# Where the split of the output weights begins, and which engine subtracts for the gating unit's first weights

## The chip, the cores and the metric

The kernel runs on one core of one Trainium2 chip. The metric is the device time of one execution in microseconds, lower being better. A core has a matrix engine (TensorE, PE in the profile; PEld is its weight load), a vector engine (VectorE, DVE), an engine for activations and copies (ScalarE, ACT), a programmable engine (GpSimd, POOL) and SyncE (SP), which here only issues transfers between the chip's memory and the on-chip buffers. Each engine takes its instructions in the order of its own queue and waits where an operand isn't there yet.

## What is computed

Two layers on 512 tokens of width 1024, all in float32. Each layer has a mixer and a dense feed-forward part, with RMS norms before and after each.

```python
def reference(x, norm_gains, ...):
    for i in range(DEPTH):                      # DEPTH = 2
        h = _rmsnorm(x, norm_gains[i, 0])
        h = _rwkv7_time_mix(h, ...) if i % 2 == 0 else _sgu_mixer(h, ...)
        x = x + _rmsnorm(h, norm_gains[i, 1])
        h = _rmsnorm(x, norm_gains[i, 2])
        h = _swiglu(h, ffn_w_gate[i], ffn_w_up[i], ffn_w_down[i])
        x = x + _rmsnorm(h, norm_gains[i, 3])
    return x

# time mixing: S_t = S_{t-1} diag(w_t) + (S_{t-1} a_t) b_t^T + v_t k_t^T ;  y_t = S_t r_t, 16 heads of 64
    ...
    return (y * g) @ w_o

# gating unit
    h = jax.nn.gelu(x @ w_in + b_in, approximate=False)
    u, v = jnp.split(h, 2, axis=-1)
    ...                                         # layer norm of v, s = masked block product of ws and v
    return (u * s) @ w_out
```

## The kernel before

**Precision.** A float32 product is made of three products of rounded halves: hi by hi, hi by lo, lo by hi (`mm3`, L206). Each weight tile therefore is loaded by SyncE into one of two `wraw` buffers (L188), cast to `whi` by ScalarE (L181) and its remainder `wlo = wraw - whi` subtracted by VectorE (L182, in `split`). With `pool=True` the cast is at L197 and GpSimd does the subtraction (L198). A `wraw` buffer is free again once its `wlo` is made.

**Stages.** The program runs through the time mixer (to about 460 us), the first FFN, the gating unit (from about 810 us, its first weights earlier), and the second FFN (from about 965 us).

**The time mixer** treats the 16 heads in four groups of four (b = 0 to 3). The recurrence is done in chunks of 64 tokens. For each group, `back(b)` inverts triangular 64 x 64 blocks, by 16 x 16 on VectorE (the loop that ends with the transposes Dn and Dt, L1054 and L1055) and then by two merges with small products on TensorE: Qp (L1071), Qs (L1074, VectorE), Np and Tp (L1080, L1083), copies to Dn2 and `bdT` (L1086, L1088), Q2p (L1094) with its copies Q2 (L1097, L1098), and T2p (L1103). The final merge is the pair of copies at L1107, by ScalarE for one head of a pair and by VectorE for the other. After it come four rounds of mp (L1112), the copy MVt (L1114, ScalarE), gh (L1119) and two sums on VectorE (L1121, L1122). The scan of group b (`scan(b)`) needs them: chunk by chunk, us (L1148), su (L1150 VectorE, L1153 ScalarE) and Yp (L1161). Its `su` tiles are four buffers in turn, each loaded by SyncE (L1133) as soon as the chunk four back is through.

**The output projection** (`out_proj`) multiplies the mixer's result `oT` by `w_o`, in units of 256 rows by 512 columns, 24 matmuls each, into four accumulators called `acc`. Its matmuls are available early, for the heads that are done, and fill gaps on TensorE during the last inverse and the last scan. The argument `after` holds traced instructions: every instruction that a unit issues on an engine is put behind those of them that are on that same engine.

**What sets the order.** The program is built with a scheduler that simulates the time line and from it chooses the order of each engine's queue. So an edge added at one place can move instructions anywhere behind it. The engines then follow the chosen order, whatever the real time.

**The gating unit** multiplies the normed rows by the second half of `w_in` first, in two halves of 512 columns with four weight units each. The normed rows `hT` come from the end of the first FFN: for each block of 128 tokens the sum of squares, then rm, rr, rt, ry on one column (L269 to L272, VectorE), the new x (L336), transposes on TensorE, and hT (L62 ScalarE, L64 VectorE).

**The second FFN** uses sums of weight blocks (wsum, L405) and of activations (tsum, split into `bc`) to save products. TensorE's accumulators there are called R, Q and Z.

Of the kernel before, what the change touches and what calls it, by code (L numbers as in the profile page):

```python
# [13 lines left out]
P = 128  # L14
T = 512
D = 1024
KT = D // P
# [115 lines left out]
class Trunk:  # L133
# [535 lines left out]
    def rwkv(self, x0):  # L669
        nc, i, tc = self.nc, self.i, self.tc  # L670
        v, a, g = nc.vector, nc.scalar, nc.gpsimd
        mm = nc.tensor.matmul
        with ExitStack() as ctx:
# [352 lines left out]
            def back(b, o):  # L1026
# [5 lines left out]
                bdT = inv[0]  # L1032
# [12 lines left out]
                for j in range(15):  # L1045
                    n = 15 - j
# [52 lines left out]
                T2p = self.bank("pt", "T2p")  # L1099
                for u in range(16):  # L1100
                    for hd in q2:
                        z = 64 * hd
                        mm(T2p[z:z + 32, u * 32:(u + 1) * 32], Q2[z + 32:z + 64, u, :], bdT[z + 32:z + 64, u, hd, 32:64],  # L1103
                           start=True, stop=True)
                for hd, cp in ((0, a.copy), (1, v.tensor_copy)):
                    z = 64 * hd
                    cp(bdT[z:z + 32, :, hd, 32:64], T2p[z:z + 32, :].rearrange("p (u t) -> p u t", t=32))  # L1107

                for hh, q in units:
                    mp, mt, mv, bx = self.bank("mp" if b else "pt", "mp"), MVt[hh, q], MV[hh, q], BX[hh, q]  # L1110
# [137 lines left out]
            xr, kr, ops, Y = None, {}, {}, {}  # L1248
            for n in PLAN:
                f, b = n[0], int(n[1])  # L1250
                if f == "P":
                    if xr is None:
                        xr = mixed_split(0, "ssssssss")
                    kr[b] = kr_proj(b)
                elif f == "E":
                    ops[b] = early(b, *kr[b])
                elif f == "X":
                    xs = mixed_split(2, XV)
                elif f == "V":
                    v_proj(xs, [b])  # L1260
                elif f == "F":
                    front(b, ops[b])
                elif f == "B":
                    back(b, ops[b])
                elif f == "S":
                    if b == 3:
                        GW.append(gate_weights(b))
                        OB.extend(bonus(b, ops[b]))
                    Y[b] = scan(b, ops[b], (lambda y: finish_half(b, ops[b], y, (0, 1))) if b == 3 else None)
                elif b == 3:  # L1270
                    finish_half(b, ops[b], Y[b], (2, 3))
                else:
                    finish(b, ops[b], Y[b])
# [15 lines left out]
            xts = [self.xp.tile([P, D], F32, name="x", tag="x", bufs=TT) for _ in range(TT)]  # L1289
            for t in range(TT):  # L1290
                nc.sync.dma_start(out=xts[t], in_=i["x"][0, t * P:(t + 1) * P, :])
            wo = i["rwkv_w_o"][0].rearrange("(u j p) n -> u p j n", p=P, j=2)
            norm = self.prenorm("g02")
            self.out_proj(acts, lambda u: wo[u], KT, i["norm_gains"][0, 1], xts, norm=norm, spare=e2, after=(ops[3]["turned"], ops[3]["copied"]))
            return xts, norm


    def sgu(self, xts, norm, nxt):
        nc, i = self.nc, self.i
        v, a, g = nc.vector, nc.scalar, nc.gpsimd  # L1300
        mm = nc.tensor.matmul
        w_in = i["sgu_w_in"][0]
# [16 lines left out]
        for half in range(2):  # L1319
            cols = slice(D + half * 512, D + half * 512 + 512)  # L1320
            hc = slice(half * 512, half * 512 + 512)
            acc = self.accs(1 - half)
            for u in range(4):
                hi, lo = self.weight(w_in.rearrange("(u j p) n -> u p j n", p=P, j=2)[u][:, :, cols], pool=half == 0)
                for j in range(2):
                    kt = 2 * u + j
                    for tt in range(TT):
                        tok = slice(tt * P, (tt + 1) * P)
                        self.mm3(acc[tt], (hT[kt][:, 0, tok], hT[kt][:, 1, tok]), (hi[:, j, :], lo[:, j, :]),
                                 kt == 0, kt == KT - 1)  # L1330
            for tt in range(TT):
                v.scalar_tensor_tensor(vt[tt][:, hc], acc[tt], norm.y[tt][:, 0:1], bv[:, hc], op0=ALU.mult, op1=ALU.add)
                s = self.sm.tile([P, 1], F32, name="vs", tag="vs", bufs=8)
                a.activation(vt[tt][:, hc], vt[tt][:, hc], AF.Gelu, accum_out=s)
                sums[half].append(s)
# [15 lines left out]
        for m in range(KT):  # L1351
            hi, lo = self.weight(w_in.rearrange("(kt p) n -> p kt n", p=P)[:, :, m * P:(m + 1) * P])
# [3 lines left out]
            u = uT[m // 2][:, m % 2, :]  # L1356
# [5 lines left out]
        acts = []  # L1362
        for m in range(8):
# [3 lines left out]
            t = self.sm.tile([P, T], F32, name="hn", tag="hn", bufs=2)  # L1367
# [6 lines left out]
        wo = i["sgu_w_out"][0].rearrange("(u j p) n -> u p j n", p=P, j=2)  # L1374
# [57 lines left out]
```

## Time and profile before

| what | us |
|---|---|
| median of 3 runs (lowest to highest) | 1325.09 (1322.51 to 1326.42) |
| the profiled execution's own time | 1323.67 |
| its span in the trace | 1322.0 |

The trace's mean granted TensorE clock is 0.979 of full speed. Times in what follows are counted from the start of the trace's span. In a row of the time line stand the start, the time, the engine, the line, the operation, output and inputs, and how many instructions the row joins; in brackets how long the engine had been idle ahead of it, and what it waited for.

### The profile page before, as it was taken

The page shows a single profiled execution, that of the slowest core. Times are in us where ns is not written, and L with a number is a line of the kernel's source. Part 1 is how long each engine was busy: PE and PEld are TensorE (multiplying, and loading weights), DVE is VectorE, ACT ScalarE, POOL GpSimd, SP SyncE. Part 2 cuts the span into 40 slices and gives each one's busy share as a digit, 9 for nine tenths or more (in the row PEclk, how much of TensorE's full clock was granted, in tenths as well). Part 3 has the DMA queues.
Part 4 walks back from the last instruction along what each step waited for, and adds up shares of the span by engine and source line. Part 5 has one row for each costly group of instructions (what it writes and reads, how often), then busy time and mean ns, then how long its engine had stood idle before and what let it go on. Part 6 is the DMA issues. An engine that isn't in the chain of part 4 may idle for free.

```text
span 1322.0 us, 24413 instructions
## 1 busy us (share of the span) xinstructions
PE 1260.2 (95%) x9644; PEld 1093.2 (83%) x9644; DVE 990.8 (75%) x1609; ACT 739.6 (56%) x1303; POOL 161.3 (12%) x304
## 2 busy tenths in 40 slices
PE   5999999989989899999999998999999999999998
PEld 3677798978867698999997877878888999998876
DVE  7975756477956687878779967476679877888985
ACT  7976884676543453445556546543454454556553
POOL 0000383566000002100000003020002000000000
PEclk9999999999889999999999999999989999999999
DMA  5137694322243225334353413343430433434322
GB/s 162 42 100 180 151 214 140 88 75 68 72 130 114 69 71 159 86 107 128 97 168 120 132 36 120 93 136 93 142 96 1 125 100 97 128 114 158 112 64 80
DMA packets 219379, 144.29 MB, mean 109 GB/s; under 512 B 67920, under 2 KB 193408, under 8 KB 219264
## 3 DMA queue, kind: packets, MB, share of 16 engines
q1 hardware_dynamic: 217968, 138.01, 36.3%
q0 software_dynamic: 1296, 4.72, 1.1%
q8 instruction: 76, 1.25, 0.4%
q14 instruction: 39, 0.32, 0.1%
HBM read 128.54 MB, written 14.16 MB: 108 GB/s over the span
## 4 chain that ended last, share of the span: by engine, by line
PE 65%; DVE 9%; ACT 2%; DMA 1%; issue 1%; SPq 0%; DVEq 0%; ACTq 0%
PE acc L206 25%; PE Q L206 10%; PE Z L206 7%; PE gu L206 7%; PE R L206 6%; PE u L206 3%; DVE wlo L182 1%; PE gh L1119 1%; DVE wsum L405 1%; PE lm L1004 1%; DVE x L336 1%; PE Yp L1161 1%; PE mp L1112 1%; DMA wraw<-in_rwkv_w_o_dram 1%; PE s L1366 1%
## 5 line engine op out<-in xcount | busy, mean ns | idle before, releaser
L182 DVE TENSOR_TENSOR wlo<-wraw,whi 128x1024 fp32r<-128x1024 f32 x79 | 98.7, 1249 | 72.2 <-ACT whi L181 71.8
L206 PE MATMUL Q<-bc,whi 128*128 128x256 f32 x816 | 147.3, 281 | 2.2 <-ACT hn L449 2.2
L206 PE MATMUL acc<-whi,ablk 128*128 128x512 f32 x448 | 141.6, 395 | 2.7 <-DVE acc L623 2.7
L181 ACT CAST whi<-wraw 128x1024 fp32r<-128x1024 f32 x79 | 82.8, 1049 | 103.2 <-PE acc L206 31.5
L206 PEld LDWEIGHTS Q<-bc,whi 128*128 128x128 f32 x816 | 125.6, 189 | 2.7 <-ACT hn L449 2.6
L181 ACT CAST whi<-wsum 128x1024 fp32r<-128x1024 f32 x68 | 71.0, 1051 | 87.6 <-DVE wsum L405 25.8
L206 PE MATMUL gu<-hT,whi 128*128 128x256 f32 (+1 forms) x448 | 112.8, 343 | 2.7 <-DVE hT L64 1.4
L206 PE MATMUL Q<-bc,wlo 128*128 128x256 f32 x408 | 114.5, 281 | 0.0
L206 PEld LDWEIGHTS acc<-whi,ablk 128*128 128x128 f32 x448 | 84.1, 188 | 23.3 <-ACT hn L621 1.8
L206 PE MATMUL Z<-bc,whi 128*128 128x256 f32 x544 | 99.8, 281 | 2.9 <-DVE bc L182 2.9
L206 PE MATMUL R<-bc,whi 128*128 128x256 f32 x544 | 98.7, 281 | 0.0
L182 DVE TENSOR_TENSOR wlo<-wsum,whi 128x1024 fp32r<-128x1024 f32 x68 | 82.2, 1220 | 19.1 <-ACT whi L181 18.1
L181 ACT CAST whi<-wq 128x1024 fp32r<-128x1024 f32 x51 | 53.5, 1050 | 76.0 <-PE gu L206 23.3
L206 PEld LDWEIGHTS gu<-hT,whi 128*128 128x128 f32 x448 | 79.5, 199 | 12.9 <-DVE hT L64 2.1
L206 PE MATMUL acc<-wlo,ablk 128*128 128x512 f32 x224 | 88.5, 395 | 1.4 <-DVE wlo L182 1.4
L206 PEld LDWEIGHTS Z<-bc,whi 128*128 128x128 f32 x544 | 84.0, 189 | 3.1 <-DVE bc L182 3.1
L206 PEld LDWEIGHTS R<-bc,whi 128*128 128x128 f32 x544 | 83.8, 188 | 0.3
L182 DVE TENSOR_TENSOR wlo<-wq,whi 128x1024 fp32r<-128x1024 f32 x51 | 63.6, 1251 | 26.9 <-ACT whi L181 26.8
L206 PE MATMUL proj<-xsp,whi 128*128 128x512 f32 x256 | 82.4, 401 | 1.3 <-ACT r L813 1.3
L206 PEld LDWEIGHTS Q<-bc,wlo 128*128 128x128 f32 x408 | 77.3, 189 | 0.0
L206 PE MATMUL R<-bc,wlo 128*128 128x256 f32 x272 | 76.6, 282 | 0.0
L206 PE MATMUL Z<-bc,wlo 128*128 128x256 f32 x272 | 76.3, 281 | 0.0
(379 smaller groups left out, 3219.3 us busy)
## 6 DMA issues: line engine op xcount, KB each, us to landing
wc<-in_ffn_w_down_dram SPq DMA_DIRECT2D x38, 512.0 KB, 3.8
wq<-in_ffn_w_gate_dram SPq DMA_DIRECT2D x68, 256.0 KB
wq<-in_ffn_w_up_dram SPq DMA_DIRECT2D x68, 256.0 KB, 4.5
wraw<-in_rwkv_w_rkv_dram SPq DMA_DIRECT2D x24, 512.0 KB, 5.2
wraw<-in_sgu_w_in_dram SPq DMA_DIRECT2D x16, 512.0 KB, 4.8
wraw<-in_ffn_w_gate_dram SPq DMA_DIRECT2D x10, 512.0 KB
wraw<-in_ffn_w_up_dram SPq DMA_DIRECT2D x10, 512.0 KB, 3.8
x<-in_x_dram SPq DMA_DIRECT2D x8, 512.0 KB, 3.3
```

The lines of the kernel that those rows point to most:

```text
L181: self.nc.scalar.copy(hi, src)
L182: self.nc.vector.tensor_tensor(lo, src, hi.bitcast(F32), op=ALU.subtract)
L206: self.nc.tensor.matmul(out, l, r, start=start, stop=stop, skip_group_check=resumed)
L336: v.scalar_tensor_tensor(xts[tt][:, c], f, y[:, 0:1], xts[tt][:, c], op0=ALU.mult, op1=ALU.add)
L405: v.tensor_tensor(s, x, y, op=ALU.add)
L1004: mm(lm[:, cc * P:(cc + 1) * P], st[:, cc].rearrange("p n t -> p (n t)"), mv[:, cc, :, hd, :], start=True, stop=True)
L1112: mm(mp[:, cc * P:(cc + 1) * P], bdT[:, q * NC + 4 * hh + cc].rearrange("p h t -> p (h t)"), mt[:, cc, :], start=True, stop=True)
L1119: mm(gh[:, cc * P:(cc + 1) * P], mt[rows, cc, :], bx[rows, 0:2, cc, :], start=True, stop=True)
L1161: mm(yp[yr, yc], MV[hh, q][:, cc, 1, hd, :], su[:, q, hd, :], start=True, stop=True)
L1366: mm(acc[:, tt * P:(tt + 1) * P], vt[tt][:, m * P:(m + 1) * P], wsT[:, m, :], start=True, stop=True)
```

## The change

Two edits. The final merge's copies at L1107 are remembered under `merged0` (ScalarE's) and `merged1` (VectorE's), and the mixer's output projection gets these two of the last group as `after`. So far it got the transpose Dt (L1055, VectorE, `turned`) and the last copy MVt at L1065 (ScalarE, `copied`), which both come before Qp. And in the gating unit the weights of the first half are no longer marked for GpSimd.

```diff
                 for hd, cp in ((0, a.copy), (1, v.tensor_copy)):
                     z = 64 * hd
-                    cp(bdT[z:z + 32, :, hd, 32:64], T2p[z:z + 32, :].rearrange("p (u t) -> p u t", t=32))
+                    o["merged" + str(hd)] = cp(bdT[z:z + 32, :, hd, 32:64], T2p[z:z + 32, :].rearrange("p (u t) -> p u t", t=32))
...
-            self.out_proj(acts, lambda u: wo[u], KT, i["norm_gains"][0, 1], xts, norm=norm, spare=e2, after=(ops[3]["turned"], ops[3]["copied"]))
+            self.out_proj(acts, lambda u: wo[u], KT, i["norm_gains"][0, 1], xts, norm=norm, spare=e2, after=(ops[3]["merged0"], ops[3]["merged1"]))
...
-                hi, lo = self.weight(w_in.rearrange("(u j p) n -> u p j n", p=P, j=2)[u][:, :, cols], pool=half == 0)
+                hi, lo = self.weight(w_in.rearrange("(u j p) n -> u p j n", p=P, j=2)[u][:, :, cols])
```

ScalarE's queue from the copy Dn2 of the last inverse to the casts behind its final merge; `whi` is the cast of an output weight, `Q_4547` is Q2, `su` and `Y` belong to the scan of group 2:

```order
 L1086 COPY Dn_4507<-Np 32x512 x2
-L1153 ACTIVATE su<-us,pc 64x64 x2
 L1088 COPY bdT<-Tp 32x16x32
 L1097 COPY Q_4547<-Q2p 32x512
-L181 CAST whi<-wraw 128x1024
 L1088 COPY bdT<-Tp 32x16x32
 L1153 ACTIVATE su<-us,pc 64x64 x2
-L181 CAST whi<-wraw 128x1024
+L1163 COPY Y<-Yp 128x256
+L1153 ACTIVATE su<-us,pc 64x64 x2
 L1107 COPY bdT<-T2p 32x16x32
+L181 CAST whi<-wraw 128x1024 x2
```

The two casts that stood ahead of the second bdT copy and of the merge copy now stand behind the latter. Two more casts that stood ahead of Qp's end have moved there as well, and the third and later ones stand between the MVt copies of the rounds.

SyncE's queue at the same place; `wraw` is the load of an output weight, `su` that of a scan tile (the last pair of group 2's and the first of group 3's), `g2r` a gate weight:

```order
 L1133 DMA su<-Vd 64x2x64 x2
-L188 DMA wraw<-in_rwkv_w_o_dram 128x2x512
-L1133 DMA su<-Vd 64x2x64 x2
 L1209 DMA g2r<-in_rwkv_g_dram 32x256 x3
-L188 DMA wraw<-in_rwkv_w_o_dram 128x2x512
-L1133 DMA su<-Vd 64x2x64 x2
-L188 DMA wraw<-in_rwkv_w_o_dram 128x2x512
-L1133 DMA su<-Vd 64x2x64 x2
+L1133 DMA su<-Vd 64x2x64 x8
+L188 DMA wraw<-in_rwkv_w_o_dram 128x2x512 x2
```

The loads of the third and the fourth output weight, which alternated with the su loads, now stand behind eight of these. The first two output weights are loaded long before in both versions.

VectorE's queue at the start of the gating unit, after the change, from the third token block's hn (`hn_9006`) to its row factor `ry_9013` and the first hT; `wlo_9260` and `wlo_9290` are two of the four remainders that GpSimd made before:

```order
L333 TENSOR_TENSOR hn_9006<-acc_8093,gain_8833 128x512
L269 TENSOR_SCALAR rm_9011<-ss_9007,rh_8858 128x1
L182 TENSOR_TENSOR wlo_9260<-wraw_9257,whi_9259 128x1024
L270 RECIPROCAL rr_9010<-rr_9010 128x1
L182 TENSOR_TENSOR wlo_9290<-wraw_9287,whi_9289 128x1024
L271 SCALAR_TENSOR_TENSOR rt_9012<-rr_9010,rm_9011 128x1
L333 TENSOR_TENSOR hn_9065<-acc_8094,gain_8833 128x512
L269 TENSOR_SCALAR rm_9070<-ss_9066,rh_8866 128x1
L270 RECIPROCAL rr_9069<-rr_9069 128x1
L272 SCALAR_TENSOR_TENSOR ry_9013<-rt_9012,rr_9010 128x1
L64 SCALAR_TENSOR_TENSOR hT_8972<-ptr_8980,vecT0_97,hT_8972 128x128
```

Before, rm, rr, rt and ry of this block followed each other, then came the two updates of x (L336) with that ry, and then the fourth block's hn, rm and rr and the first hT. Now two remainders stand among them and the two updates of x behind the first four hT. The third remainder stands some instructions ahead of this piece, the fourth behind the last ry.

VectorE's queue in the second FFN before the change, from one act product to the next; `bc_10956` is the remainder of a sum of activations, `wsum_11224` the sum of two weight blocks that are loaded there:

```order
L426 TENSOR_TENSOR act_10877<-sg_10944,R_10881 128x256
L405 TENSOR_TENSOR wsum_11224<-wq_11218,wq_11221 128x1024
L405 TENSOR_TENSOR wsum_11060<-wsum_11060,wq_10913 128x1024
L182 TENSOR_TENSOR bc_10956<-tsum_10953,bc_10955 128x1024
L405 TENSOR_TENSOR wsum_11287<-wq_10985,wq_11218 128x1024
```

And after it:

```order
L426 TENSOR_TENSOR act_10877<-sg_10944,R_10881 128x256
L405 TENSOR_TENSOR wsum_11060<-wsum_11060,wq_10913 128x1024
L182 TENSOR_TENSOR bc_10956<-tsum_10953,bc_10955 128x1024
L405 TENSOR_TENSOR wsum_11224<-wq_11218,wq_11221 128x1024
L405 TENSOR_TENSOR wsum_11287<-wq_10985,wq_11218 128x1024
```

`wsum_11224` has moved behind `bc_10956`. On TensorE the acc matmuls that lay between Qp and T2p, and between T2p and the first mp, have moved behind the first mp's start, all but one of them.

## The prediction, made before the changed kernel was timed

> **What bounds the kernel now.** I read the first part of the page, then windows of the stages, then the timeline engine by engine at each place the change touches. Last I read TensorE's waits.
>
> ```profile
> PE 1260.2 (95%) x9644; PEld 1093.2 (83%) x9644; DVE 990.8 (75%) x1609; ACT 739.6 (56%) x1303; POOL 161.3 (12%) x304
> 358.00:400.00 42.00, 35.77 (x673) 29.18 (x660) 23.13 (x46) 18.70 (x39) 1.11 (x3) 0.92 0.46 135
> 400.00:440.00 40.00, 39.43 (x249) 31.22 (x248) 21.59 (x47) 13.01 (x30) 0.00 (x0) 1.00 0.33 108
> ```
>
> TensorE is busy 95% of the span, so only its idle time and its stretches below full clock can be won. The windows (columns: length, then busy time of PE, PEld, DVE, ACT, POOL, then granted clock, DMA share, GB/s) show where that stands around the last inverse: 6.2 of 42 us idle at clock 0.92, then almost none. Whatever the stage gains by 400 us therefore lasts to 440. The change touches three such pockets: A, this inverse; B, the start of the gating unit; C, one place in the second FFN that only the scheduler moves.
>
> **A, the last inverse (355 to 420 us).** The inverse is a latency chain: Qp, Qs, Np and Tp, Q2p, T2p, the merge copies, then four rounds of mp, MVt, gh.
>
> ```profile
> 357.71 1.29 PE L1071 MATMUL Qp<-hn,LA 32*32 32x32 f32 x128
> 370.50 1.04 ACT L181 CAST whi<-wraw 128x1024 fp32r<-128x1024 f32 x1 [1.04 <-DMA wraw<-in_rwkv_w_o_dram]
> 371.56 0.58 ACT L1088 COPY bdT<-Tp 32x512 f32<-32x512 f32 x1
> 373.23 1.20 PE L1103 MATMUL T2p<-bdT,Q 32*32 32x32 f32 x64
> 376.83 1.04 ACT L181 CAST whi<-wraw 128x1024 fp32r<-128x1024 f32 x1 [4.15 <-DMA wraw<-in_rwkv_w_o_dram]
> 377.90 0.57 ACT L1107 COPY bdT<-T2p 32x512 f32<-32x512 f32 x1
> 382.86 1.16 PE L1112 MATMUL mp<-MVt,bdT 128*128 128x128 f32 x8
> 385.48 1.71 PE L1119 MATMUL gh<-BX,MVt 64*128 64x128 f32 x16 [0.85 <-ACT MVt L1114]
> 396.72 1.71 PE L1119 MATMUL gh<-BX,MVt 64*128 64x128 f32 x16
> ```
>
> Twice a cast of an output weight stands on ScalarE ahead of a copy of the inverse and waits for its load: 1.04 us before the bdT copy that T2p needs, 4.15 us before the merge copy. The change removes exactly this. Without the first cast (its 1.04 of wait and 1.04 of work) T2p comes about 2.1 us sooner, at 371.1. Without the second, ScalarE's merge copy (0.57) follows T2p's end (372.3) at once and ends at 372.9, where before it ended at 378.5. In the new order the first cast (1.04) and an acc matmul that needs it stand ahead of the first mp, so mp starts at about 374.0, where before it was 382.86: 8.9 us sooner.
>
> Not all of that is won. In the new order, no acc matmul runs between Qp and T2p any more; 33 of the 34 that run before the last gh now stand between the first mp and that gh, where none stood. Two of them at full clock and two at half clock:
>
> ```profile
> 398.94 0.63 PE L206 MATMUL acc<-whi,oT 128*128 128x512 f32 x2
> 399.41 0.39 PE L206 MATMUL acc<-wlo,oT 128*128 128x512 f32 x1
> 370.88 1.05 PE L206 MATMUL acc<-whi,oT 128*128 128x512 f32 x2
> 328.00:338.00 10.00, 10.00 (x131) 8.42 (x131) 9.63 (x25) 7.09 (x15) 3.90 (x8) 0.50 0.35 113
> 370.00:372.00 2.00, 2.00 (x5) 1.61 (x6) 1.13 (x3) 1.48 (x2) 0.41 (x2) 0.50 0.08 19
> 374.00:376.00 2.00, 2.00 (x46) 1.75 (x39) 0.00 (x0) 0.00 (x0) 0.00 (x0) 1.00 0.76 249
> ```
>
> At full clock two start 0.47 us apart (398.94 to 399.41), so 0.235 each; a pair takes 0.42 us more at half clock, 0.21 each. From the first mp to the end of the last gh before took 15.6 us (382.86 to 398.43), 0.85 of it the wait shown at gh, which an acc matmul now fills. After: 374.0 + 15.6 − 0.9 + 33 × 0.235 = 396.5, that is 1.9 us sooner, with 34 acc matmuls done where before had 24, so 10 × 0.235 = 2.3 less to do later. Gross gain 4.2 us.
>
> Two costs come off. **The clock**: with nothing but 32x32 and 64-wide matmuls from 359 to 372, I expect half clock to be granted when the acc matmuls begin. Before, the clock was at 0.50 from 370 to 372, though acc matmuls had begun, and full by 374; so I take 2.5 us at half, worth 1.2 us. By the rows this price has bounds of 0 and 5.0, the latter from the stretch 328 to 338 (the inverse before this one), where half clock lasted 10 us though TensorE is shown busy throughout. The Trainium skill, "TensorE: Matmul & The Clock Gate", section "What's actually happening", says the clock is halved after an idle window of about 3.4 us and full again after about 3.4 us of sustained activity; by it the price would be 1.7 us, so A 0.5 us smaller. The row 328 to 338 speaks against so short a recovery. **The third load**: SyncE takes its queue in order.
>
> ```profile
> 372.82 0.39 SPq L188 DMA_DIRECT2D wraw<-in_rwkv_w_o_dram  x1
> 383.00 2.87 SPq L1133 DMA_DIRECT2D su<-Vd  x4
> ```
>
> The load of the third output weight now stands behind eight su loads, and needs the wraw buffer that the first wlo frees. The last of those su loads waits for scan 2's chunk 6, which before let it go only at 383.00 and now stands on TensorE right behind T2p, at about 373. The first wlo ends at about 375.3, so the load issues then and lands 4.0 later (372.82 to 376.83), at 379.3. Its cast stands on ScalarE ahead of the second MVt and ends at 380.4; the mp that this MVt needs ends at about 381 (gh 2.6 us behind mp as before, 11 acc matmuls in place of the wait, then gh and mp). So nothing is lost by the rows, but the cover is thin, and I put 0.3 us. Behind these loads on SyncE stand su and hn loads which scan 3 needs only after 400, so they cost nothing unless the third load slips (third rival).
>
> A: −4.2 + 1.2 + 0.3 = **−2.7 us**; bounds −4.2 and +1.1 (clock price 5.0).
>
> **B, start of the gating unit (798 to 825 us).**
>
> ```profile
> L182 DVE TENSOR_TENSOR wlo<-wraw,whi 128x1024 fp32r<-128x1024 f32 x79 | 98.7, 1249 | 72.2 <-ACT whi L181 71.8
> 809.03 4.71 POOL L198 TENSOR_TENSOR wlo<-wraw,whi 128x1024 fp32r<-128x1024 f32 x2 [8.24 <-ACT whi L197]
> 818.08 2.37 POOL L198 TENSOR_TENSOR wlo<-wraw,whi 128x1024 fp32r<-128x1024 f32 x1 [1.40 <-ACT whi L197]
> 809.29 1.05 ACT L197 CAST whi<-wraw 128x1024 fp32r<-128x1024 f32 x1
> 807.19 0.16 DVE L272 SCALAR_TENSOR_TENSOR ry<-rt,rr 128x1 f32<-128x1 f32 x1
> 809.63 1.80 DVE L271 SCALAR_TENSOR_TENSOR rt<-rr,rm 128x1 f32<-128x1 f32 x1
> 811.47 2.29 DVE L272 SCALAR_TENSOR_TENSOR ry<-rt,rr 128x1 f32<-128x1 f32 x1
> 815.12 0.68 DVE L333 TENSOR_TENSOR hn<-acc,gain 128x512 f32<-128x512 f32 x1
> 815.91 1.11 DVE L64 SCALAR_TENSOR_TENSOR hT<-ptr,vecT,hT 128x128 fp32r<-128x128 f32 x4
> 818.10 2.37 DVE L272 SCALAR_TENSOR_TENSOR ry<-rt,rr 128x1 f32<-128x1 f32 x1
> 816.30 1.22 PE L206 MATMUL acc<-whi,hT 128*128 128x512 f32 x2 [3.44 <-DVE hT L64]
> 800.00:805.00 5.00, 5.00 (x24) 4.05 (x23) 1.40 (x5) 1.96 (x6) 0.79 (x1) 1.00 0.33 110
> 810.00:815.00 5.00, 2.86 (x21) 2.27 (x19) 4.93 (x4) 3.86 (x13) 3.74 (x2) 1.00 0.34 111
> 815.00:820.00 5.00, 3.70 (x10) 2.90 (x11) 5.00 (x14) 3.99 (x10) 2.50 (x2) 0.66 0.59 204
> ```
>
> Three VectorE instructions on one column, of 0.16 us at 807.19, last 1.80, 2.29 and 2.37, each while GpSimd runs one of the four subtracts and ending with it: about 6.0 us beyond that in which VectorE is held off, and it is the engine that TensorE waits for (3.44 us), at a clock of 0.66 afterwards. The change takes the subtracts off GpSimd and adds four of 1.25 to VectorE, 5.0 in all. One of these falls in 800 to 805, where VectorE is busy 1.40 of 5 us. Two stand between the third row block's L269 and L271, where the two long rows are gone; the last stands behind the last ry.
>
> Worked through in the new order from 809.5, just ahead of the first long row: two wlo are 2.5 (the second's cast ends at 810.34, in time); hn, rm and rr 0.8, as from 815.12 to 815.91; the other rr, rt and ry some 0.5. So the first hT starts at about 813.3 instead of 815.91. The two x updates (L336) that stood ahead of it now stand behind it. TensorE starts 2.6 us sooner, and with under 1 us idle instead of 3.44 the clock need not fall: (1 − 0.66) × 3.70 = 1.3 us more. Against that I put 0.4 us for x and the next hT coming tighter behind one wlo. B: −2.6 − 1.3 + 0.4 = **−3.5 us**; bounds −5.0 (nothing given back, the third long row worth a little more) and −1.0 (6.0 against 5.0, all serial).
>
> **C, second FFN (1028 to 1037 us).** Nothing in the diff speaks of it, but the order moves.
>
> ```profile
> 1029.58 0.41 DVE L426 TENSOR_TENSOR act<-sg,R 128x256 f32<-128x256 f32 x1
> 1032.62 1.23 DVE L405 TENSOR_TENSOR wsum<-wq 128x1024 f32<-128x1024 f32 x1 [2.62 <-DMA wq<-in_ffn_w_up_dram]
> 1033.76 1.22 DVE L405 TENSOR_TENSOR wsum<-wsum,wq 128x1024 f32<-128x1024 f32 x1
> 1034.90 1.22 DVE L182 TENSOR_TENSOR bc<-tsum,bc 128x1024 fp32r<-128x1024 f32 x1
> 1032.94 0.28 PE L206 MATMUL Q<-bc,wlo 128*128 128x256 f32 x1
> 1036.17 0.39 PE L206 MATMUL Z<-bc,whi 128*128 128x256 f32 x1 [2.95 <-DVE bc L182]
> ```
>
> The subtract for bc stands behind a sum that waits 2.62 us for a load; TensorE stands still 2.95 us for bc. In the new order the sum that waits stands behind bc. The second sum and bc then take 1029.95 to 1032.3, while TensorE's Q runs to 1033.2: the whole wait is covered. The sums behind are as early as before, and their casts and subtracts are due about 3 us sooner relative to TensorE, for which I give back 0.1. C: **−2.8 us**, bounds −2.95 and 0.
>
> **The sum.** −2.7 − 3.5 − 2.8 = −9.0 us. The profiled execution took 1323.67 us (span 1322.0), 1.4 below the median of 1325.09; on the median the same gain gives 1316.1, and I say **1316**. The other engines' orders are nearly the same elsewhere, so I put nothing there.
>
> **Rivals.**
> 1. **The clock eats A.** The acc matmuls that went are the only full-width ones between Qp and T2p. If half clock lasts 10 us, as at 328 to 338, A is +1.1 and the time 1325.1 + 1.1 − 3.5 − 2.8 = 1319.9. For: that row. Against: recovery by 374 before.
> 2. **VectorE stays the bound at B.** It is busy 4.93 and 5.00 of 5 us there, and 5.0 us are added against 6.0 removed. If all of it is serial, B is −1.0, and the time 1318.6. Against: one subtract falls into idle time and two x updates go behind hT.
> 3. **Slower: the third output weight comes late.** Its cast is ahead of the second MVt and its subtract ahead of the first gh sums, so each us of issue later than 376 moves three gh rounds by one, and a new standstill of TensorE costs up to 3.4 more (16 acc matmuls by 0.21) at half clock. With B and C as forecast, the gain is used up if the load issues at about 382 to 385, and it is slower by over 4 us from about 386 to 389. Before, the su loads now ahead of it went out at 383.00; 390 would give −9.0 + 14.0 + 3.4, or 1333. For: SyncE's queue is in order. Against: chunk 6 of scan 2 stands right behind T2p now, so it would have to be 10 us late by a wait that I don't see.
> 4. **The scheduler's gain at C is not there**, because the order follows simulated landings and another load binds next: C is 0, time 1318.9.
>
> **How the numbers follow.** Forecast 0.50, rivals 0.15, 0.12, 0.10 and 0.08, and 0.05 for two of the first, second and fourth together (about 1322). The range takes A, B and C to their good ends (−12.2, so 1313) with 3 us for the spread of runs (1322.5 to 1326.4), and at the other end everything short of the third rival: 1310 to 1325. About 0.3%, or 4 us, is what a measurement of this kernel can tell from no change. Faster by more than that: most of the forecast and of rivals 1, 2 and 4, 0.71; within it 0.18; slower 0.11.
>
> **What would show it.** A: in the timeline, no cast between Qp and the merge copies, the first mp at 374 rather than 383, the third wraw issue at 376, clock windows near 0.5 for 2 to 3 us from 372, the last gh near 396.5 with 34 acc matmuls done. B: L271 and L272 all near 0.2 us, TensorE's wait for the first hT under 1 us, clock 1.00. C: no wait of Z for bc at the place. It is wrong if TensorE waits between the first and second gh for a w_o load, if the clock stays at half past 380, or if the first Z wait comes back as a wait of another product within 10 us.

## The result and the profile after

The changed kernel took **1315.96 us** in the median of five runs (1312.98 to 1320.0), the kernel before 1325.44 (1322.51 to 1326.76). The ratio is 0.9933, 95% interval 0.9911 to 0.9956. The profiled execution took 1315.28 us with a span of 1313.6. So the forecast of 1316 was met, but in part by luck: of its three terms C was met, B came out better, and A, the inverse, brought little of what was forecast.

To see where the time went I cut each trace at the start of four rows: Qp of the last inverse, the first gu of the first FFN, the first wst of the gating unit, and its first s.

| stretch | before | after | difference | forecast |
|---|---|---|---|---|
| start to Qp | 357.71 | 356.53 | −1.2 | 0 |
| Qp to gu (place A) | 102.30 | 101.71 | −0.6 | −2.7 |
| gu to wst | 350.48 | 351.22 | +0.7 | 0 |
| wst to s (place B) | 99.94 | 95.39 | −4.5 | −3.5 |
| s to end (place C) | 411.57 | 408.75 | −2.8 | −2.8 |

**Place A.** First the timeline of the changed kernel, ScalarE's casts and copies and SyncE's load, then TensorE's rows:

```profile
371.89 0.57 ACT L1107 COPY bdT<-T2p 32x512 f32<-32x512 f32 x1 [0.95 <-PE T2p L1103]
372.49 1.99 ACT L181 CAST whi<-wraw 128x1024 fp32r<-128x1024 f32 x2
380.51 1.04 ACT L181 CAST whi<-wraw 128x1024 fp32r<-128x1024 f32 x1 [0.88 <-DMA wraw<-in_rwkv_w_o_dram]
383.33 0.59 ACT L1114 COPY MVt<-mp 128x512 f32<-128x512 f32 x1 [1.78 <-PE mp L1112]
361.36 13.27 SPq L1133 DMA_DIRECT2D su<-Vd  x8
374.82 1.53 SPq L188 DMA_DIRECT2D wraw<-in_rwkv_w_o_dram  x2
356.53 1.29 PE L1071 MATMUL Qp<-hn,LA 32*32 32x32 f32 x128
365.08 1.92 PE L1094 MATMUL Q2p<-Dn,LA 32*32 32x32 f32 x64 [0.18 <-ACT Dn L1086]
374.19 1.91 PE L1112 MATMUL mp<-MVt,bdT 128*128 128x128 f32 x8
397.27 1.71 PE L1119 MATMUL gh<-BX,MVt 64*128 64x128 f32 x16
```

No cast of an output weight stands ahead of the merge copy any more. From Qp to the first mp it is now 17.7 us, before 25.2. The third weight's load issued at 374.82, its cast waited for the landing, and the second MVt waited for its mp and not for that cast. Yet the last gh starts at 397.27, where it had been 396.72. The reason shows in the windows of the whole stretch and of pieces of it. The columns are the length, then busy time of PE, PEld, DVE, ACT and POOL, then granted clock, DMA share and GB/s. Before, Qp to gu, and two pieces of it:

```profile
357.71:460.01 102.30, 91.36 (x1002) 72.91 (x1000) 59.54 (x136) 43.05 (x100) 1.11 (x3) 0.95 0.35 108
368.00:372.00 4.00, 4.00 (x62) 3.46 (x57) 2.46 (x5) 2.54 (x4) 0.41 (x2) 0.61 0.40 137
380.00:384.00 4.00, 4.00 (x29) 2.97 (x28) 0.45 (x2) 0.78 (x4) 0.00 (x0) 0.68 0.38 131
```

After, the same stretch, and five pieces of it:

```profile
356.53:458.24 101.71, 92.93 (x1002) 75.47 (x1000) 59.96 (x136) 43.31 (x100) 1.10 (x3) 0.92 0.35 109
360.00:364.00 4.00, 2.91 (x180) 2.77 (x181) 1.53 (x4) 2.15 (x6) 0.00 (x0) 0.63 0.33 73
364.00:368.00 4.00, 3.34 (x90) 3.14 (x90) 1.65 (x3) 2.52 (x5) 0.00 (x0) 0.50 0.06 12
368.00:372.00 4.00, 4.00 (x89) 3.64 (x89) 0.98 (x2) 1.72 (x7) 0.41 (x2) 0.50 0.13 28
372.00:376.00 4.00, 3.75 (x27) 3.27 (x25) 3.33 (x4) 2.97 (x5) 0.00 (x0) 0.50 0.20 29
376.00:380.00 4.00, 4.00 (x17) 2.96 (x17) 0.35 (x1) 0.96 (x2) 0.00 (x0) 0.74 0.73 257
```

TensorE's idle time fell from 10.9 to 8.8 us (length less busy time), but the loss by the clock, busy time by one less the granted clock, rose from about 4.6 to 7.4 (7.8 with the clock unrounded). Half clock held from about 361 to 378, 17.1 us in one piece. Before, the clock had fallen too, but came back sooner: 3.4 us from 368.9, again 3.4 us from 379.1, and 3.4 us from 444.

**Place B.** The timeline of the changed kernel, VectorE and then TensorE, and two windows:

```profile
808.42 1.22 DVE L182 TENSOR_TENSOR wlo<-wraw,whi 128x1024 fp32r<-128x1024 f32 x1
809.63 1.21 DVE L182 TENSOR_TENSOR wlo<-wraw,whi 128x1024 fp32r<-128x1024 f32 x1
810.75 0.21 DVE L271 SCALAR_TENSOR_TENSOR rt<-rr,rm 128x1 f32<-128x1 f32 x1
811.67 0.14 DVE L272 SCALAR_TENSOR_TENSOR ry<-rt,rr 128x1 f32<-128x1 f32 x1
811.74 1.13 DVE L64 SCALAR_TENSOR_TENSOR hT<-ptr,vecT,hT 128x128 fp32r<-128x128 f32 x4
812.14 0.73 PE L206 MATMUL acc<-whi,hT 128*128 128x512 f32 x2 [0.30 <-DVE hT L64]
810.00:815.00 5.00, 4.70 (x29) 3.78 (x28) 5.00 (x16) 4.85 (x15) 0.54 (x1) 1.00 0.75 228
815.00:820.00 5.00, 5.00 (x25) 4.10 (x24) 4.76 (x18) 5.00 (x19) 0.00 (x0) 1.00 0.57 195
```

The long rows are gone, TensorE waits 0.30 us for the first hT instead of 3.44, and the clock stays at 1.00 where it was 0.66. VectorE is as full as before, now with work of its own.

**Place C.** VectorE's timeline in the second FFN, and TensorE's first Z that needs bc:

```profile
1024.78 1.22 DVE L405 TENSOR_TENSOR wsum<-wsum,wq 128x1024 f32<-128x1024 f32 x1
1025.92 1.22 DVE L182 TENSOR_TENSOR bc<-tsum,bc 128x1024 fp32r<-128x1024 f32 x1
1027.05 2.35 DVE L405 TENSOR_TENSOR wsum<-wq 128x1024 f32<-128x1024 f32 x2
1027.93 0.28 PE L206 MATMUL Z<-bc,whi 128*128 128x256 f32 x1
```

bc comes ahead of the sum that had waited, and Z runs without a wait in brackets.

### The profile page after: what moved, and what is told of

It reads as the page before. It is cut to its first block, busy times and chain, and to the rows that moved or that the text cites. A ratio compares the mean times of both kernels' runs of the same rounds, so it can differ in the third digit from the quotient of the medians.

```text
span 1313.6 us, 24404 instructions
## 1 busy us (share of the span) xinstructions
PE 1257.4 (96%) x9644; PEld 1091.1 (83%) x9644; DVE 988.1 (75%) x1613; ACT 739.4 (56%) x1303; POOL 151.6 (12%) x300
## 4 chain that ended last, share of the span: by engine, by line
PE 68%; DVE 7%; ACT 2%; issue 1%; DMA 1%; POOL 0%; DVEq 0%; ACTq 0%
PE acc L206 25%; PE Q L206 10%; PE gu L206 9%; PE R L206 7%; PE Z L206 7%; PE u L206 3%; DVE wlo L182 1%; PE gh L1119 1%; PE mp L1112 1%; PE Yp L1161 1%; PE lm L1004 1%; DVE wsum L405 1%; DVE x L336 1%; PE s L1366 1%; PE ptr L281 0%
## 5 line engine op out<-in xcount | busy, mean ns | idle before, releaser
L182 DVE TENSOR_TENSOR wlo<-wraw,whi 128x1024 fp32r<-128x1024 f32 x83 | 103.1, 1244 | 66.5 <-ACT whi L181 57.7
L181 ACT CAST whi<-wraw 128x1024 fp32r<-128x1024 f32 x83 | 86.9, 1050 | 101.5 <-PE acc L206 29.2
L206 PE MATMUL Z<-bc,whi 128*128 128x256 f32 x544 | 99.8, 281 | 0.0
L206 PEld LDWEIGHTS gu<-hT,whi 128*128 128x128 f32 x448 | 78.8, 197 | 13.7 <-ACT hT L62 2.4
```

Source lines behind the costliest of these rows:

```text
L181: self.nc.scalar.copy(hi, src)
L182: self.nc.vector.tensor_tensor(lo, src, hi.bitcast(F32), op=ALU.subtract)
L206: self.nc.tensor.matmul(out, l, r, start=start, stop=stop, skip_group_check=resumed)
```

## The experiments

**Each part alone, and more work for TensorE in the gap.** My theory from the two traces: part 1 wins time in the inverse and gives it back at half clock, since it takes away the only full-width products between Qp and T2p; B and C carry the result. The rival: part 1 is worth what the forecast said.

The first run has only part 1 (shown against the changed kernel):

```diff
-                hi, lo = self.weight(w_in.rearrange("(u j p) n -> u p j n", p=P, j=2)[u][:, :, cols])
+                hi, lo = self.weight(w_in.rearrange("(u j p) n -> u p j n", p=P, j=2)[u][:, :, cols], pool=half == 0)
```

> Only the output weights' split behind the merge copies; the gating unit as before (GpSimd subtracts for its first half). bc stands ahead of the waiting sum in the second FFN here too. Theory 1 (what part 1 wins in the chain it gives back at half clock): from Qp's start to the first gu of the first FFN 101.7 us as in the changed kernel (before 102.3), half clock for over 12 us within 358 to 380, GpSimd's long rows at the gating unit still there, the wait of Z for bc gone; time 3 to 4 us under before. Rival (part 1 is worth the 2.7 us of the forecast, the rest was luck): Qp to gu about 99.6, time 5.5 under before.

It took 1320.64 us (12 runs; before beside it 1326.80 in 17), ratio 0.9965 (0.9946 to 0.9985): 4.6 us under before by the ratio, give or take 2.6, and 6.2 by the medians. Qp to gu was 101.8 with 17.1 us at half clock, s to end 408.9. As C alone is 2.6 in this trace, some 2 us are left for A, with an interval that holds both 0 and the forecast. The stage and its clock speak for the theory, the time for neither.

The second has only part 2:

```diff
-            self.out_proj(acts, lambda u: wo[u], KT, i["norm_gains"][0, 1], xts, norm=norm, spare=e2, after=(ops[3]["merged0"], ops[3]["merged1"]))
+            self.out_proj(acts, lambda u: wo[u], KT, i["norm_gains"][0, 1], xts, norm=norm, spare=e2, after=(ops[3]["turned"], ops[3]["copied"]))
```

> Only the gating unit's subtracts on VectorE; the output weights' split as before. bc stands ahead of the waiting sum here too. Theory 1: Qp to gu 102.3 as before, first gu to the first s matmul of the gating unit 446.6 (before 450.4), from there to the end 408.8 (before 411.6); time 6.5 to 7.5 us under before, so hardly slower than the whole change. Rival (part 1 matters): 6.3 under before or less, and 2.7 us slower than the whole change run beside it.

The time was 1316.17 us (6 runs), the ratio 0.9924 (0.9898 to 0.9950), against 0.9924 (0.9898 to 0.9951) for the whole change on the same chip. That is some 10 us under before, where both theory and rival had said 7.5 at most. With B and C there, part 1 adds nothing that can be seen; but the six runs of each spread over 6 us, and by that spread I estimate that a gain of up to some 3 us could hide in it, so these times alone don't rule out the 2.7 of the forecast. Its profile held a surprise, though, in the windows of Qp to gu and of one piece:

```profile
355.32:463.45 108.13, 98.35 (x1002) 79.64 (x1000) 60.33 (x136) 43.16 (x100) 1.10 (x3) 0.87 0.33 102
384.00:396.00 12.00, 12.00 (x67) 10.76 (x65) 7.17 (x16) 2.85 (x6) 0.69 (x1) 0.50 0.40 133
```

In this execution the old order got half clock for 6.8 us from 365.1, as long as the two falls of before took together in the inverse, and then for 17.1 us more from 382.1, while TensorE was shown busy all through. The stretch took 108.1 instead of the expected 102.3. The same queue can end on either side, so a difference of single traces in this stage, A's −0.6 too, says little by itself. I take this as one source of the scatter of before, whose 17 runs beside these went from 1319.75 to 1331.31; that the other runs differ by this was not traced.

The third is the test of the clock by useful work. The first two weight units, loaded long before, keep the old points; the later ones go behind the merge copies (called two units early below):

```diff
-                for ins in after:
+                for ins in (after[0:2] if half == 0 and u < 2 else after[2:4] or after):
                     order.enter_context(self.tc.issue_after(ins.ins))
...
-after=(ops[3]["merged0"], ops[3]["merged1"])
+after=(ops[3]["turned"], ops[3]["copied"], ops[3]["merged0"], ops[3]["merged1"])
```

> The whole change, but the first two units of output weights, whose loads have landed long before, stay behind the old points (Dt, MVt) and only the later units go behind the merge copies. So full-width acc matmuls lie again between Qp and T2p and no cast that waits for a load stands ahead of a copy of the inverse. Theory 1 (it was the clock): half clock for under 6 us between Qp and the second gh, first mp within 17 us of Qp's start (17.7 in the changed kernel, 25.2 before), Qp to gu 99 or less, time 2 to 3 us under the whole change. Rival (the chain of the inverse was not the limit, scan 3 is): Qp to gu 101.5 to 102.5 whatever the clock, time as the whole change.

```profile
358.86:458.04 99.18, 89.90 (x1003) 72.53 (x1001) 59.75 (x136) 42.53 (x101) 1.10 (x3) 0.98 0.36 112
368.00:372.00 4.00, 3.30 (x100) 3.12 (x100) 2.18 (x4) 1.87 (x5) 0.09 (x1) 0.72 0.48 143
372.00:376.00 4.00, 4.00 (x82) 3.13 (x82) 0.45 (x2) 1.06 (x5) 0.32 (x2) 0.85 0.09 21
```

These windows are Qp to gu and the only two pieces below full clock: in sum 3.4 us at half (0.28 and 0.15 of 4 us, by two), where the change's trace had 17.1. TensorE's idle time is 9.3 us, no less than the change's 8.8; what has gone is most of the clock's loss, from 7.4 to 1.8. The time was 1311.54 us (1310.20 to 1312.29), ratio 0.9888 (0.9864 to 0.9911), and its slowest run is under the change's fastest (1313.27 beside it). That is 4.3 us under the change run beside it, more than the 2 to 3 expected. The first mp came 18.8 us after Qp, later than the 17 expected and than the change's 17.7, and the stage was shorter all the same. Not all of the 4.3 need lie in this stage: from gu to wst this trace is 3.0 us shorter than that of the change beside it, which has 6.8 us at half clock there and this one none.

The fourth was the change itself, on the same chip.

> The changed kernel itself, beside the others on the same chip, for the comparison and for the spread of its stages from run to run: 8 to 10 us under before, Qp to gu 101.2 to 102.2, half clock from about 361 to 378 again.

It took 1315.82 us (1313.27 to 1319.65), 10.1 us under before by the ratio. Qp to gu was 103.2, 1 us over what I expected; half clock came from 364.4 to 378.0, 13.7 us instead of 17. Qp started at 359.3 instead of 356.5: the traces of one kernel are up to 3 us apart before the inverse begins. One difference shows in all twelve traces of this case: the six in which Qp starts at 358.9 or later have a piece of half clock between 79 and 85 us (granted clock 0.72 there in this run), and the six in which it starts at 357.7 or earlier have none (1.00 in the change's first trace). Why the clock falls there in some executions is open.

**Work without use in the gap.** If it is the missing full-width work, products that nobody reads should keep the half clock short too. 28 were put where TensorE idles, once as products and once as transposes:

```diff
                 Qp = self.bank("pt", "Qp")
...
+                def filler(n):
+                    if b == 3:
+                        fill = self.ps.tile([P, 512], F32, name="fill", tag="b2", bufs=1)
+                        for k in range(n):
+                            mm(fill[:, 0:P], self.ident, self.ident, start=True, stop=True)
+
+                filler(8)
                 Qs = el("Qs", (P, 16, 32))
...
+                filler(10)
                 Q2p = self.bank("pt", "Q2p")
...
+                filler(10)
                 T2p = self.bank("pt", "T2p")
```

> The changed kernel with 28 products of the 128x128 identity by itself (float32, result never read) between Qp and T2p: 8 after Qp, 10 ahead of Q2p, 10 ahead of T2p, where TensorE is idle in the changed kernel. Nothing else is moved. Theory 1 (half clock comes of the missing full-width work): half clock for under 8 us within 356 to 384 (17 us in the changed kernel), Qp to first gu 100 or less though work is added, time 1 to 3 us under the whole change. Rival (half clock there depends on the small products themselves or on nothing here): half clock as long as in the changed kernel, Qp to gu 102 to 104, time 0 to 2 us over it.

Timeline and windows of it, first the three rows of filler (each product is two instructions):

```profile
360.59 2.05 PE L1077 MATMUL fill<-ident 128*128 128x128 f32 x16
368.13 3.60 PE L1077 MATMUL fill<-ident 128*128 128x128 f32 x20
373.20 2.50 PE L1077 MATMUL fill<-ident 128*128 128x128 f32 x20
359.37:463.39 104.02, 96.45 (x1059) 77.80 (x1057) 59.77 (x136) 42.91 (x100) 1.10 (x3) 0.98 0.34 106
```

The clock came out as expected (0.98 over the stretch, 3.4 us at half), the time did not: Qp to gu was 104.0, as the rival had it, and the kernel took 1317.96 us, ratio 0.9940 (0.9922 to 0.9959), no better than the change. The filler itself takes 8.2 us and lengthens the chain: Qp to mp is 20.1 us instead of 17.7. So full-width work in the gap keeps the half clock short, but here it paid only where it was work that had to be done anyway.

> The same 28 at the same places, but as transposes of the identity. In the kernel before, the stretch 328 to 338 was at half clock though TensorE ran 128x128 transposes through most of it. If transposes don't count as the full-width work that holds the clock: half clock for over 12 us and Qp to gu 102 to 104, while the products of the other run shorten it. If they count: as the products, within 0.5 us.

```profile
372.00:380.00 8.00, 8.00 (x134) 6.98 (x134) 1.67 (x3) 2.00 (x5) 0.33 (x2) 0.53 0.01 2
```

With transposes this 8 us window was nearly all at half clock, part of a piece of 10.2 us from 369.4, and the stretch had 0.94 on average, between the change's 0.92 and the products' 0.98. Qp to gu was 105.6, over both forecasts, in what was the slowest of the eight runs. But a transpose is one instruction and a product two, so there was also half as much work. Whether transposes count less as such stays open. The time was 1318.14 us (1311.92 to 1322.19), the ratio 0.9931 (0.9908 to 0.9955).

**GpSimd's hold.** Two of its four subtracts put back:

```diff
-[u][:, :, cols])
+[u][:, :, cols], pool=half == 0 and u in (1, 2))
```

> The changed kernel, but GpSimd again subtracts for the second and third unit of the gating unit's first half (L198 there twice instead of four times). If it is GpSimd's subtract that holds VectorE off: one or two of rt and ry (L271, L272) last over 1 us again, TensorE waits about 3 us for the first hT again, wst to s 98.5 to 100 (95.2 to 95.4 in the changed kernel, 99.9 before), time 3 to 4.5 us over the whole change. Rival (the order of the queue made the gain, not the hold): no long rows, wst to s 95 to 96.

```profile
807.46 4.72 POOL L198 TENSOR_TENSOR wlo<-wraw,whi 128x1024 fp32r<-128x1024 f32 x2 [47.70 <-ACT whi L197]
807.75 0.20 DVE L269 TENSOR_SCALAR rm<-ss,rh 128x1 f32<-128x1 f32 x1
807.87 0.15 DVE L270 RECIPROCAL rr<-rr 128x1 f32<-128x1 f32 x1
808.06 1.81 DVE L271 SCALAR_TENSOR_TENSOR rt<-rr,rm 128x1 f32<-128x1 f32 x1
809.90 2.30 DVE L272 SCALAR_TENSOR_TENSOR ry<-rt,rr 128x1 f32<-128x1 f32 x1
814.74 0.74 PE L206 MATMUL acc<-whi,hT 128*128 128x512 f32 x2 [3.45 <-DVE hT L64]
```

Everything of before is back: both long rows, ending with GpSimd's two, the wait of 3.45 us, and wst to s at 100.1. The order of VectorE's queue went back with it, so the time alone would not separate the hold from the order; the two rows do, with 3.8 us over their length in the changed kernel. The time was 1320.73 us, ratio 0.9965 (0.9950 to 0.9979), 4.8 over the change's 1315.96, which was not timed beside it, and 4.2 by the ratios. The Trainium skill, "GPSIMD Engine Reference", section "Specifications", says that GpSimd shares its interfaces to the on-chip memory with VectorE and contends with VectorE instructions that have two inputs there. The trace agrees: rt and ry have two such inputs and were held, while rm and rr, with one (rm's rh is a single value per row, not a second tensor), took their usual 0.20 and 0.15 us within the first subtract.

**One unit early, and C by itself.** In this version the scheduler happened to put the waiting sum ahead of bc again.

```diff
-                for ins in after:
+                for ins in (after[0:2] if half == 0 and u < 1 else after[2:4] or after):
```

> As the run with two units early, but only the first unit stays behind the old points. In this version the scheduler puts the sum that waits for its load ahead of bc again, as before the change. If that order is what C is: TensorE waits 2.5 to 3 us for bc at one place in the second FFN, and s to the end is 411 to 412 (408.3 to 409.1 in the four kernels with bc ahead). For the clock: 6 full-width matmuls between Qp and T2p instead of 12, so Qp to gu between the 99.2 with two and the 101.7 to 103.2 with none. Time 1314 to 1317.

```profile
1030.72 1.22 DVE L405 TENSOR_TENSOR wsum<-wq 128x1024 f32<-128x1024 f32 x1 [2.62 <-DMA wq<-in_ffn_w_up_dram]
1034.27 0.38 PE L206 MATMUL Z<-bc,whi 128*128 128x256 f32 x1 [2.95 <-DVE bc L182]
```

The wait came back to the hundredth, and s to end is 411.5, where the ten other traces from the changed kernel on, all with bc ahead, have 407.6 to 409.1. Qp to gu was 103.3, no gain over the change, with half clock for 10.2 us from 370.7, and the time 1322.34 us, ratio 0.9978 (0.9957 to 0.9998), more than I expected. C explains 2.8 of the 6.4 us over the change. In the profiled execution the rest lies ahead of Qp (3.3 us later) and in Qp to gu (1.6 longer); whether it does so in the other runs is open.

The clock here suggests where full-width products help. The six of this run stand ahead of the fall (362.0 to 364.4). With two units early six more ran right behind the fall (371.6 to 374.0 in the first trace), and half clock lasted 3.4 us there and 6.8 in the two later traces of that order.

**The version that beats both, again.** First the third run's kernel once more, then the same with GpSimd's subtract for the first unit alone (`pool=half == 0 and u == 0`).

> The version with two units early once more, to see whether its time and its small spread hold: 1310 to 1313, half clock again for under 6 us within 356 to 384, and less than 3 us between its fastest and slowest run (6 to 7 us in the whole change).

It took 1310.40 us (1309.34 to 1313.11), ratio 0.9891 (0.9871 to 0.9911). Half clock was some 7 us this time, a little over the forecast, and Qp to gu 99.8, so the stage is shorter than the change's 101.7 and 103.2 in both traces of this order. The spread of 3.8 us was over the 3 I expected.

> The same, but GpSimd subtracts for the first unit of the gating unit's first half, at a time when VectorE is idle over half of the time; TensorE's order is the same. If GpSimd's subtract costs only where VectorE has two-input work at the same time: rt and ry short, wst to s 95 to 95.5, time within 1 us of the other. If it costs wherever it stands: wst to s longer by 1 to 2.

It took 1313.19 us, ratio 0.9911 (0.9895 to 0.9927). Its stages are those of the other: Qp to gu 99.8, wst to s 95.2, no long row, as expected for a subtract at an idle time. But the time is 2.8 over, and in its trace Qp starts at 359.2 instead of 355.9, in a part whose order is the same; it is one of the six with half clock between 79 and 85 us. Since the stages behind are equal, I don't put that on GpSimd; for the other four runs it stays open.

## Why the prediction came out as it did

- **A, the step that failed: "so I take 2.5 us at half, worth 1.2".** The chain was right in kind: casts of output weights gone from it, the first mp 7.5 us sooner after Qp (8.9 forecast), the third load at 374.82 (375.3) and without harm. But half clock came 4.5 us after Qp, during the small products, and held 17.1 us. I had dated it from the first acc matmuls and taken its length from 370 to 372 of before, where full-width products ran; I had also overlooked the second fall of before, from 379.1. In the trace the stage was about 3.7 us longer than the sum without its two costs, which were 1.2 for the clock and 0.3 for the load. Some 1.4 of that lies ahead of the first mp (17.7 us after Qp for 16.3 forecast; Q2p and T2p took 1.92 and 1.91 us, before 1.20 each). Some 2.3 lies between it and the end of the last gh (24.8 us for 22.5), of which the first 3.9 us were at half clock. So A was −0.6 in the traces instead of −2.7, and the times of part 2 alone and of the whole change show no difference.
- **The first rival** had the mechanism and a price nearer to it: 5.0 us for 10 us of half clock, against about 3.7 for 17. Its time of 1319.9 didn't come: A was −0.6 in the traces and not +1.1, and B and the stretch ahead of Qp were better than it assumed. The sign "half past 380" missed the case by 2 us, since full clock was back at 378.1.
- **The cause** is shown by two units early: with full-width work back in the gap, half clock lasts 3.4 and 6.8 us in the two traces, Qp to gu is 99.2 and 99.8, and the time 4.3 us under the change run beside it. The filler products, put into that gap of the changed kernel, cut the half clock to 3.4 us as well.
- **The rule weighed at that place** (the Trainium skill, "TensorE: Matmul & The Clock Gate", section "What's actually happening": full clock after about 3.4 us of sustained activity) also gave too short a time here: from 368 to 376 TensorE was busy 7.75 of 8 us at 0.50. Full clock came 1 to 2 us after the 128x512 matmuls ran one behind the other, at 378.
- **B: right in mechanism, mis-sized.** −4.5 for −3.5. The first hT came 3.1 us sooner relative to wst (2.6 forecast), and the 0.4 us given back for the work behind it wasn't needed. That it was mostly GpSimd's hold and not the new order is shown by the two long rows that came back with two subtracts on GpSimd. The second rival (VectorE's 5.0 added against 6.0 removed, all serial) fell.
- **C: right, −2.8 for −2.8**, and the fourth rival fell. It belongs to no part of the change: it came with part 1 alone and with part 2 alone, and went with one unit early.
- **The third rival**, the late load, didn't come: the eight su loads were through by 374.6.
- The sum was met by luck. In the trace A was 2.1 us worse and B 1.0 better than forecast, the stretch ahead of Qp 1.2 better and gu to wst 0.7 worse, and neither of these last two was forecast. No edit touches what runs ahead of Qp; there the trace before has 23.9 us at half clock and that of the changed kernel 10.2.

## What to carry to other kernels

When work is moved out of a gap to shorten a chain, look at what else it did there: with full-width products in a gap of small ones TensorE's half clock lasted 3.4 to 6.8 us (two units early), without them 13.7 to 17.1, and the chain's gain went into that. Move only what makes the chain wait (here the casts that wait for loads) and leave what is ready. And where a scheduler orders the queues, look for the waits it happens to remove or bring back far from the edit: 2.8 us of this result hung on the order of two VectorE instructions over 200 us behind the nearer edit.

## What the runs showed of the hardware

- Half clock doesn't end by TensorE being busy: it lasted 17.1 us over rows that are busy throughout (from 382.1, with gh, mp and some scan products, in the run with part 2 alone; 384 to 396 is shown above, 12.00 of 12 us at 0.50).
- In these traces idle time goes ahead of it. In Qp to gu of the twelve traces the clock falls 19 times, at least once in each, with full-width products in the gap or without. Each time TensorE had been busy for only 0.31 to 0.64 of the 3.41 us just ahead, and each half clock lasted 3.4 us or two to five times that. So the full-width products did not prevent the fall; they shortened what followed it. Two such pieces ahead of a fall, of the changed kernel and then of the first run with two units early:

```profile
357.61:361.02 3.41, 1.97 (x98) 1.79 (x86) 1.22 (x3) 0.40 (x1) 0.00 (x0) 1.00 0.71 204
366.36:369.77 3.41, 1.07 (x74) 1.07 (x75) 1.19 (x3) 1.49 (x4) 0.00 (x0) 1.00 0.44 104
```

- A VectorE instruction on one column with two inputs in the on-chip memory (rt, ry) that starts during a GpSimd subtract lasts until that subtract ends (1.81 and 2.30 us for 0.14 to 0.21), as if it were stopped and not merely slowed. Those with one such input (rm, rr) are not held (0.20 and 0.15 us).
